# Moving the later SBUF pools to multiples of 512 bytes, and the second chunk of narrow weight units to byte 2048

## The chip, the cores and the metric

The kernel runs on one core of a Trainium2 chip (trn2). The metric is the device time of one execution in microseconds, as the median of several runs. Before the change it is 2218.45 us (three runs, 2217.58 to 2218.74).

A core has a matrix engine (TensorE, PE in the profile), two engines for elementwise work (VectorE, DVE, and ScalarE, ACT), a general one (GpSimd, POOL) and a queue processor (SyncE, SP). All read an on-chip memory, SBUF, of 128 partitions; an operand's place in it is the byte at which it begins in each partition. TensorE writes to PSUM, an accumulation memory. A matmul has a stationary operand, which a weight load (LDWEIGHTS, PEld in the profile) brings into the array, and a moving operand, whose columns stream through it.

## The reference, cut to what matters

The program is a two-layer decoder trunk on 256 tokens of width 2048, all in float32:

```python
for i in range(DEPTH):                       # 2 layers
    if i == N_A_LAYERS:                      # i == 1
        fk, fv, fc = fox_shared_kv(x, fox_kv_norm, fox_w_kv, fox_b_f)
    mk, mv = memory_kv(mem_n, mem_w_kv[i])
    h = rmsnorm(x, norm_mix[i])
    if i < N_A_LAYERS:  x = x + gla_mixer(h, mk, mv, gla_w_in[i], ..., gla_w_out[i])
    else:               x = x + fox_mixer(h, fk, fv, fc, mk, mv, fox_w_in[j], fox_w_out[j])
    h = rmsnorm(x, norm_ffn[i])
    x = x + conv_ffn(h, ffn_w_up[i], ffn_conv_w[i], ffn_conv_b[i], ffn_w_down[i])
return rmsnorm(x, norm_final)
```

`conv_ffn` multiplies by a 2048 x 11264 matrix, applies a causal convolution of width 3 over the tokens, a gate, and multiplies by a 5632 x 2048 matrix. The mixers are a gated linear attention (GLA, 4 heads, keys of 256, values of 384) and a forgetting attention (FoX, 12 heads of 128), each with four heads that attend to 256 memory tokens. Nearly all arithmetic is the product of 256 tokens with some 104 million weights, each of which is read once from the main memory.

## The kernel before, in words

**Arithmetic.** Every weight and every activation is split into a high and a low part (`hi`, `lo`), both of a type called float32r that the matrix engine takes in one pass. A product is three matmuls: high by high, low by high, high by low. The tokens stand as the stationary operand, 128 tokens by 128 channels at a time, and the weights move, up to 512 columns at a time.

**Weights.** The weights lie in the main memory as units (`_layout`, line 114 on). A unit of most panels holds two chunks of 128 input channels (`per` = 2) by n output columns, side by side in each partition: chunk 0 in columns 0 to n - 1, chunk 1 in columns n to 2n - 1. `split_unit` (line 209) issues one DMA for a unit into a buffer `raw` (four of them), one ACT instruction that rounds it into `whi`, and one DVE instruction that subtracts to give `wlo`. `whi` and `wlo` have four buffers of 4096 bytes (`NUNIT` = 1024 columns) each, so PE can be up to four units behind.

**Panels.** A panel is a block of output columns. `panel_tm` (line 307) makes one step for each of its eight units: 12 matmuls, over two blocks of 128 tokens, two chunks, and the three products. n is 512 in most panels. It is 384 in four of them (three of the GLA value panels, `("gv", 1)` to `("gv", 3)`, and `("fv", 3)`). It is 400 in `("gv", 0)` (384 values and 16 gate columns, 8 units), and 388 in `("fv", 0)` to `("fv", 2)` (24 units). Only 400 and 388 are no multiples of P = 128; there chunk 1 begins at byte 1600 and 1552 of its buffer.

**FFN.** `pair_steps` (line 377) runs the products of the two FFNs. Some pairs of its units are computed with seven block products in place of eight. The sums of token blocks which that needs are stationary operands; they lie in tiles `usum` and `dsum`, made by `held` (line 1375) in the pool that is handed to `ffn`. For the hidden activations 20 tiles are needed (`RING`), 16 of them in the constant pool. The other four are, in the first FFN, parts of two tiles of the constant pool (`moremk`, `moremv`, line 1635), and in the second FFN four tiles `more` in its own pool `store` (line 1703). `rows_tm` (line 338), which runs the last panels of the second FFN, reads the `more` tiles too.

**Where the tiles lie.** Pools are laid one behind the other. The constant pool and the weight pool come first. All tiles that matmuls read there (the activations `A`, `B`, `mix`, the `moremk` and `moremv` tiles, `whi`, `wlo`) begin at multiples of 512 bytes: `whi` and `wlo` fill bytes 101,376 to 134,143. The pool `small` (tiles of norms and softmax sums, `sm`, line 156) begins at byte 134,144, which is 262 x 512, and takes 5,504 bytes. So each pool that opens behind it (`load`, `near`, `gla`, `stash`, `turn1`, `fnear`, `fox`, `turn2`, `store`) begins at byte 139,648 or is stacked on one that does, and that is 272 x 512 + 384. The tiles `usum`, `dsum` and `more` all lie at 384 bytes behind a multiple of 512, and each 128 x 128 stationary operand (512 bytes in a partition) in them too. `x` and `raw` lie in a pool of the other end (`rear`) and are not concerned.

**Order.** PE's instructions run in the order in which the program gives them, within bounds: a scheduler orders all engines' instructions by priority (`tc.high_priority(offset=AHEAD)` brings a unit's load and split forward by 300 places) and by modelled costs (`schedule_with_timeline_sim=True` where the kernel is built). `tc.issue_after` ties some instructions behind others.

Of the kernel before, what the change touches and what calls it, by code (L numbers as in the profile page):

```python
# [13 lines left out]
F32 = mybir.dt.float32  # L14
F32R = mybir.dt.float32r
I32 = mybir.dt.int32
AF = mybir.ActivationFunctionType
ALU = mybir.AluOpType
PSUM = bass.MemoryType.PSUM

P = 128
# [22 lines left out]
NUNIT = 1024  # L44
# [102 lines left out]
def _trunk(ctx: ExitStack, tc: tile.TileContext, xt, xtok, memt, wp, wgu, gns, gfin, cnv, par, msk, out):  # L147
    nc = tc.nc
    where, _ = _layout()
    V, S, TE = nc.vector, nc.scalar, nc.tensor  # L150
# [3 lines left out]
    rear = ctx.enter_context(tc.tile_pool(name="rear", bufs=1, side="right"))  # L154
    x = [rear.tile([P, 2, 512], F32, name=f"x{f}") for f in range(4)]
    sm = ctx.enter_context(tc.tile_pool(name="small", bufs=2))
    pacc = ctx.enter_context(tc.tile_pool(name="pacc", bufs=4, space=PSUM))
    dram = ctx.enter_context(tc.tile_pool(name="turnd", bufs=1, space=bass.MemoryType.DRAM))
    pwork = ctx.enter_context(tc.tile_pool(name="pwork", bufs=1, space=PSUM))
# [8 lines left out]
    part = const.tile([P, P], F32, name="part")[:, :C_N]  # L168
# [15 lines left out]
    loads, casts, lows, ends, last_mm, sent = [], [], [], [], [], []  # L184
# [5 lines left out]
    def work(tag, bufs=1):  # L190
        return pwork.tile([P, 512], F32, name="ps_" + tag, tag=tag, bufs=bufs)
# [17 lines left out]
    def split_unit(unit, pieces=1, before=None):  # L209

        off, kcs, n = unit
        w = len(kcs) * n
        with tc.high_priority(offset=AHEAD):
            raw = rear.tile([P, NUNIT], F32, name="raw", tag="raw", bufs=4)
            hi = wpool.tile([P, NUNIT], F32R, name="whi", tag="whi", bufs=4)
            lo = wpool.tile([P, NUNIT], F32R, name="wlo", tag="wlo", bufs=4)
            src = wp[off : off + P * w].rearrange("(p n) -> p n", p=P)
            for i in range(pieces):
                s = slice(i * w // pieces, (i + 1) * w // pieces)
                loads.append(nc.sync.dma_start(raw[:, s], src[:, s]))  # L220
            for i in range(pieces):
                s = slice(i * w // pieces, (i + 1) * w // pieces)
                if before is not None:
                    before(i)
                casts.append(S.activation(hi[:, s], raw[:, s], AF.Copy))  # L225
                lows.append(V.tensor_tensor(lo[:, s], raw[:, s], hi[:, s].bitcast(F32), ALU.subtract))  # L226
        return hi, lo
# [6 lines left out]
    def panels_fm(keys, src, evacs, turns, between=None):  # L234

        units = [where[key] for key in keys]

        acc = [[work("s", 2) if p == 1 else pacc.tile([P, 512], F32, name="acc", tag="acc") for _ in range(2)]
               for p in range(len(keys))]
        base = min(min(u[1]) for u in units[0])  # L240
        ready = {}
        for at, (p, u, low) in enumerate(turns):
            if (p, u) not in ready:
                ready[p, u] = split_unit(units[p][u])
                if u == 1 and between is not None:
                    between()
            end = all(t[0] != p for t in turns[at + 1 :])
            w = ready[p, u][low]
            for j, kc in enumerate(units[p][u][1]):
                both = src[kc - base]  # L250
                for c in range(2):
                    s = slice(j * 256 + c * P, j * 256 + (c + 1) * P)
                    if low:
                        mm = TE.matmul(acc[p][c][:, :T], w[:, s], both[:, 0, :], start=False, stop=end and j == 3)  # L254
                    else:
                        mm = TE.matmul(acc[p][c], w[:, s], both, start=u == j == 0, stop=end and j == 3)  # L256
            if end:
                ends.append(mm)
                with tc.high_priority(offset=2 * AHEAD if len(keys) > 1 and p == 0 else 0):
                    for c in range(2):  # L260
                        evacs[p](c, acc[p][c])
# [46 lines left out]
    def panel_tm(key, src, evac, second=False):  # L308

        units = where[key]
        n = units[0][2]
        base = min(min(u[1]) for u in units)
        acc = []
        end = len(units) - 1

        def step(i):
            if i == 0:
                acc.extend(work("s", 2) if second else pacc.tile([P, 512], F32, name="acc", tag="acc")  # L320
                           for _ in range(2))
            ready = split_unit(units[i])
            passes = [(b, low) for low in range(2) for b in range(2)]
            if i == end:
                passes.sort()
            for b, low in passes:
                for j, kc in enumerate(units[i][1]):
                    for part in range(2 - low):
                        mm = TE.matmul(acc[b][:, :n], src[kc - base][:, part, b * P : (b + 1) * P],  # L329
                                       ready[low][:, j * n : (j + 1) * n], start=i == low == part == j == 0,  # L330
                                       stop=i == end and low == 1 and j == len(units[i][1]) - 1)
                if i == end and low:
                    ends.append(mm)
                    evac(b, acc[b][:, :n])
            last_mm.append(mm)

        return step
# [405 lines left out]
    with tc.tile_pool(name="load", bufs=1) as lp:  # L743
# [48 lines left out]
        def mem_keys(l, z):  # L792
            with tc.issue_after(loads[-1].ins):
                keys_far.pop(0)(flat(z))
            with tc.issue_after(lows[-1].ins):
                for k in range(MEM_H):
                    V.tensor_tensor(by_run(mk[l][:, k, :]), z[:, :, k], by_run(nrm.row()), ALU.mult)

        step = panel_tm(("mk", 0), bufA, turn_out(sq_y, keys_far.append))
        xf = [lp.tile([P, T], F32, name=f"xf{i}") for i in range(KC)]  # L800
        for u in range(8):
# [11 lines left out]
        with tc.issue_after(nrm.made.ins):  # L813
            for i in range(KC):
                split(bufB, i, xf[i], gain("mix0", i))
        step = panel_tm(("mk", 1), bufA, turn_out(sq_y, keys_far.append))
        for u in range(8):
            step(u)
            if u == 3:
# [3 lines left out]
                for f in range(4):  # L823
                    for b in range(2):
                        nx.add(f, b)
        step = panel_tm(("mv", 1), bufA, mv_out(1))
        for u in range(8):
            step(u)
# [743 lines left out]
    def preparing(name, dst, pool, far, kept=None, tag="blk", queue=nc.sync):  # L1572

        n = StreamNorm()
        blocks, rooms, turned_blocks = {}, {}, []
        away, landed = [], []  # L1580

        def land(z=None):

            f, back = away.pop(0)
            if z is None:
                z = pool.tile([P, 4, 4, 2, 32], F32, name="turn", tag="turn", bufs=2) if kept is None else kept[f]
            with tc.issue_after((loads if queue is nc.sync else sent)[-1].ins):
                back(flat(z))
            landed.append((f, z))

        def take():

            f, z = landed.pop(0)
            with tc.issue_after(casts[-1].ins):
                for k in range(4):
                    split_turned(dst, 4 * f + k, z, name)

        def then(f, b):
            n.add(f, b)
            with tc.high_priority(offset=AHEAD):  # L1600
                if b == 0:
                    blocks[f] = rooms[f]() if f in rooms else pool.tile([P, 4, 4, 2, 32], F32, name="blk", tag=tag, bufs=2)
                y = blocks[f]
                turned_blocks.append(V.transpose(y[:, :, :, b, :],
                                                 x[f][:, b, :].rearrange("p (k c i) -> p c k i", c=4, i=32)))
                if b:
                    with tc.issue_after(sent[-1].ins) if queue is nc.gpsimd else nullcontext():
                        away.append((f, far_away(far, flat(y), T, queue)))

        n.rooms = then.rooms = rooms  # L1610
        then.turned = turned_blocks
        n.land = then.land = land
        n.take = then.take = take
        return n, then

    n = gla(nx)
# [20 lines left out]
    with tc.tile_pool(name="turn2", bufs=1) as tp:  # L1637
        n, then = preparing("ffn1", bufA, tp, dram)
# [136 lines left out]
```

## Time and profile before

| what | value |
|---|---|
| median of three runs | 2218.45 us (2217.58 to 2218.74) |
| the profiled execution's own time | 2218.68 us |
| its span, first to last instruction | 2216.9 us |
| PE busy | 2205.0 us, 99% of the span, 10323 matmuls |
| DVE, ACT, POOL busy | 1784.6, 1420.0, 136.9 us (81%, 64%, 6%) |
| mean granted clock of PE | 0.999 |
| moved by DMA | 515.41 MB, 232 GB/s on the mean |

The profiled execution stands 0.23 us above the median of the runs. PE's busy time is the union of its matmuls, and each matmul's record lasts longer than the distance to the next one's start, since they are pipelined. So PE counts as busy even where its matmuls come at a slower pace; what a matmul costs is the distance between starts, which the timeline gives: start, duration of a merged row, count.

### The profile page before, as it was taken

The page shows a single profiled execution, that of the slowest core. Times are in us where ns is not written, and L with a number is a line of the kernel's source. Part 1 is how long each engine was busy: PE and PEld are TensorE (multiplying, and loading weights), DVE is VectorE, ACT ScalarE, POOL GpSimd, SP SyncE. Part 2 cuts the span into 40 slices and gives each one's busy share as a digit, 9 for nine tenths or more (in the row PEclk, how much of TensorE's full clock was granted, in tenths as well). Part 3 has the DMA queues.
Part 4 walks back from the last instruction along what each step waited for, and adds up shares of the span by engine and source line. Part 5 has one row for each costly group of instructions (what it writes and reads, how often), then busy time and mean ns, then how long its engine had stood idle before and what let it go on. Part 6 is the DMA issues. An engine that isn't in the chain of part 4 may idle for free.

```text
span 2216.9 us, 30032 instructions
## 1 busy us (share of the span) xinstructions
PE 2205.0 (99%) x10323; PEld 1854.6 (84%) x10323; DVE 1784.6 (81%) x2640; ACT 1420.0 (64%) x2255; POOL 136.9 (6%) x257
## 2 busy tenths in 40 slices
PE   9999999999999999999999999999999999999998
PEld 7888888888888888888888998888888888888886
DVE  7768977688897878888978669668888788888896
ACT  6655664566787568656765555455787657665874
POOL 0000000001100000001110000000101000100000
PEclk9999999999999999999999999999999999999999
DMA  9877567877777567667678767777777757766674
GB/s 339 253 228 225 185 199 221 262 233 254 229 242 262 186 221 242 223 223 253 219 246 264 231 199 243 228 241 247 217 238 247 243 183 249 232 247 216 223 258 150
DMA packets 165713, 515.41 MB, mean 232 GB/s; under 512 B 20716, under 2 KB 41976, under 8 KB 165560
## 3 DMA queue, kind: packets, MB, share of 16 engines
q1 hardware_dynamic: 148488, 460.99, 63.1%
q0 software_dynamic: 16496, 51.71, 7.6%
q8 instruction: 81, 1.33, 0.2%
q10 hardware_dynamic: 576, 0.79, 0.1%
q14 instruction: 72, 0.59, 0.1%
HBM read 469.62 MB, written 43.79 MB: 232 GB/s over the span
## 4 chain that ended last, share of the span: by engine, by line
PE 99%; DMA 0%; DVE 0%; ACT 0%; SPq 0%; issue 0%; DVEq 0%
PE acc L403 30%; PE acc L329 26%; PE ps_s L403 15%; PE ps_o L403 8%; PE ps_t L403 7%; PE acc L301 3%; PE acc L256 3%; PE acc L359 2%; PE ps_s L329 2%; PE acc L254 1%; PE ps_s L1014 0%; DMA raw<-wp 0%; PE ps_o L687 0%; PE ps_s L687 0%; PE ps_o L1242 0%; PE ps_s L1287 0%
## 5 line engine op out<-in xcount | busy, mean ns | idle before, releaser
L226 DVE TENSOR_TENSOR wlo<-raw,whi 128x1024 fp32r<-128x1024 f32 (+4 forms) x739 | 875.6, 1193 | 255.7 <-ACT whi L225 236.3
L225 ACT ACTIVATE whi<-raw 128x1024 fp32r<-128x1024 f32 (+4 forms) x739 | 763.7, 1041 | 442.2 <-PE acc L329 158.5
L329 PE MATMUL acc<-whi,B 128*128 128x512 f32 (+3 forms) x1248 | 291.8, 370 | 0.0
L373 ACT ACTIVATE whi<-raw 128x1024 fp32r<-128x1024 f32 (+1 forms) x136 | 129.8, 954 | 189.3 <-PE acc L403 70.4
L329 PEld LDWEIGHTS acc<-whi,B 128*128 128x128 f32 x1248 | 227.0, 188 | 28.0
L374 DVE TENSOR_TENSOR wlo<-raw,whi 128x1024 fp32r<-128x1024 f32 (+1 forms) x136 | 147.8, 1089 | 58.9 <-ACT whi L373 55.9
L403 PE MATMUL acc<-whi,mix 128*128 128x512 f32 x764 | 194.8, 389 | 0.0
L403 PE MATMUL acc<-whi,B 128*128 128x512 f32 x750 | 192.7, 389 | 0.0
L403 PEld LDWEIGHTS acc<-whi,mix 128*128 128x128 f32 x764 | 143.4, 188 | 30.0
L403 PEld LDWEIGHTS acc<-whi,B 128*128 128x128 f32 x750 | 140.8, 188 | 29.4
L329 PE MATMUL acc<-wlo,B 128*128 128x512 f32 (+3 forms) x624 | 158.5, 369 | 0.0
L329 PEld LDWEIGHTS acc<-wlo,B 128*128 128x128 f32 x624 | 114.6, 188 | 14.5
L1393 ACT ACTIVATE tap<-yzu,cw 128x256 f32<-128x256 f32 x264 | 123.6, 532 | 2.8 <-DMA yzu<-far 2.7
L1393 ACT ACTIVATE tap<-fvt,cw 128x256 f32<-128x256 f32 x264 | 123.6, 533 | 1.9 <-DMA fvt<-far 1.9
L1400 DVE TENSOR_TENSOR tap<-tap,tap 128x1024 f32<-128x1024 f32 x88 | 107.0, 1216 | 1.1 <-ACT tap L1393 1.0
L403 PE MATMUL acc<-wlo,mix 128*128 128x512 f32 x382 | 107.4, 389 | 0.0
L403 PE MATMUL acc<-wlo,B 128*128 128x512 f32 x375 | 107.1, 389 | 0.0
L403 PE MATMUL ps_s<-whi,mix 128*128 128x512 f32 x386 | 105.9, 389 | 0.0
L403 PE MATMUL ps_s<-whi,B 128*128 128x512 f32 x342 | 93.3, 389 | 0.0
L403 PEld LDWEIGHTS ps_s<-whi,mix 128*128 128x128 f32 x386 | 72.5, 188 | 15.2
L403 PEld LDWEIGHTS acc<-wlo,mix 128*128 128x128 f32 x382 | 71.8, 188 | 15.0
L403 PEld LDWEIGHTS acc<-wlo,B 128*128 128x128 f32 x375 | 70.4, 188 | 14.7
(498 smaller groups left out, 3792.6 us busy)
## 6 DMA issues: line engine op xcount, KB each, us to landing
raw<-wp SPq DMA_DIRECT2D x743, 512.0 KB, 4.5
fvt<-far POOLq DMA_DIRECT2D x100, 128.0 KB, 5.4
raw<-wp SPq DMA_DIRECT2D x32, 384.0 KB, 3.5
far<-yu POOLq DMA_DIRECT2D x22, 512.0 KB, 5.6
far<-yzu POOLq DMA_DIRECT2D x22, 512.0 KB, 5.2
yzu<-far POOLq DMA_DIRECT2D x88, 128.0 KB, 5.5
raw<-wp SPq DMA_DIRECT2D x24, 388.0 KB, 4.1
x<-xtok SPq DMA_DIRECT2D x8, 512.0 KB, 7.2
```

The costliest lines, as they stand in the source:

```text
L225: casts.append(S.activation(hi[:, s], raw[:, s], AF.Copy))
L226: lows.append(V.tensor_tensor(lo[:, s], raw[:, s], hi[:, s].bitcast(F32), ALU.subtract))
L254: mm = TE.matmul(acc[p][c][:, :T], w[:, s], both[:, 0, :], start=False, stop=end and j == 3)
L256: mm = TE.matmul(acc[p][c], w[:, s], both, start=u == j == 0, stop=end and j == 3)
L301: mm = TE.matmul(acc[b][:, :n], src[kcs[j] - base][:, part, b * P : (b + 1) * P], w, start=u == 0 and low == part == j == 0, stop=u == end ...
L329: mm = TE.matmul(acc[b][:, :n], src[kc - base][:, part, b * P : (b + 1) * P], ready[low][:, j * n : (j + 1) * n], start=i == low == part = ...
L359: mm = TE.matmul(acc[b][:, :n], src[kc - base][:, part, b * P : (b + 1) * P], w, start=i == low == part == j == 0, stop=i == end and low = ...
L373: casts.append(S.activation(hi[:, :n], src, AF.Copy))
L374: lows.append(V.tensor_tensor(lo[:, :n], src, hi[:, :n].bitcast(F32), ALU.subtract))
L403: r = TE.matmul(bank[name], x, w, start=name not in begun, stop=last)
L1393: S.activation(by_run(taps[i][:, s, c, i:]), zs[slot][:, :, 2 * c + s], AF.Copy if i else AF.Identity, bias=0.0 if i else w[3], scale=w[2 ...
L1400: V.tensor_tensor(taps[0], taps[0], taps[n][:, :, :, :T], ALU.add)
```

## The change

Two things are changed, and nothing in the arithmetic.

1. A tile `even` of 32 float32 columns (128 bytes in a partition) that nobody writes or reads is put first into the pool `small`. The pool's other tiles move up by 128 bytes, and it ends at byte 139,776 = 273 x 512. Every pool behind it moves up by 128 bytes.
2. In units whose n is no multiple of 128 (400 and 388), `split_unit` writes chunk 1 of `whi` and `wlo` to column 512, byte 2048, and `panel_tm` reads it there. The ACT and the DVE instruction stay one each, with the same elements; their output (and DVE's second input) is now two runs of n columns, 512 apart. The load is the same. `room` is NUNIT // 2 = 512 for such a unit and n for all others.

```diff
     sm = ctx.enter_context(tc.tile_pool(name="small", bufs=2))
+    sm.tile([P, 32], F32, name="even", tag="even", bufs=1)
...
                 loads.append(nc.sync.dma_start(raw[:, s], src[:, s]))
+            if n % P:
+                a, b, c = (t.rearrange("p (j m) -> p j m", j=len(kcs))[:, :, :n] for t in (raw[:, :w], hi, lo))
+                casts.append(S.activation(b, a, AF.Copy))
+                lows.append(V.tensor_tensor(c, a, b.bitcast(F32), ALU.subtract))
+                return hi, lo
             for i in range(pieces):
...
         n = units[0][2]
+        room = NUNIT // len(units[0][1]) if n % P else n
         base = min(min(u[1]) for u in units)
...
                         mm = TE.matmul(acc[b][:, :n], src[kc - base][:, part, b * P : (b + 1) * P],
-                                       ready[low][:, j * n : (j + 1) * n], start=i == low == part == j == 0,
+                                       ready[low][:, j * room : j * room + n], start=i == low == part == j == 0,
                                        stop=i == end and low == 1 and j == len(units[i][1]) - 1)
```

## The prediction

> **What bounds the kernel now.** I read the page first, then the work of each engine by stage, then PE's groups by tile, and last the timeline of single stretches of PE, which gives its pace.
>
> ```profile
> span 2216.9 us, 30032 instructions
> ...
> PE 2205.0 (99%) x10323; PEld 1854.6 (84%) x10323; DVE 1784.6 (81%) x2640; ACT 1420.0 (64%) x2255; POOL 136.9 (6%) x257
> ...
> PE 99%; DMA 0%; DVE 0%; ACT 0%; SPq 0%; issue 0%; DVEq 0%
> ...
> PE acc L301 <- ACT whi L225: 1.3, 1, 1.3
> ...
> 400.00:800.00 400.00, 400.00 (x1763) 330.64 (x1762) 329.01 (x422) 263.05 (x400) 27.41 (x50) 1.00 0.71 233
> ...
> 1600.00:2000.00 400.00, 400.00 (x1760) 330.21 (x1759) 337.43 (x398) 276.27 (x414) 35.13 (x64) 1.00 0.69 231
> ```
>
> The chain that ended last is PE for 99%. Among PE's waits the one that a split caused lasted 1.3 us, at the start. In the two stretches of 400 us, which hold most of both FFNs, PE is busy throughout at the full granted clock (the 1.00), while DVE has 329 and 337 us of work and ACT 263 and 276. So the time is the number of matmuls times their pace. Only what changes that pace, or makes a matmul wait, counts. The pace is not the same everywhere:
>
> ```profile
> 887.43 1.98 PE L403 MATMUL acc<-whi,moremk 128*128 128x512 f32 x8
> ...
> 898.31 0.39 PE L403 MATMUL acc<-whi,mix 128*128 128x512 f32 x1
> ...
> 1926.97 2.03 PE L403 MATMUL acc<-whi,more 128*128 128x512 f32 x8
> ...
> 1938.13 0.62 PE L403 MATMUL acc<-whi,mix 128*128 128x512 f32 x2
> ```
>
> Between the first two starts lie 4 units of 12 matmuls, with `moremk` and `moremv` as stationary operands: 10.88 us / 48 = 226.7 ns each. Between the last two lie the same 48 matmuls of the second FFN, from the same line, with `more`: 11.16 / 48 = 232.5 ns. The first tiles begin at multiples of 512 bytes, the second 384 bytes behind one. The difference is 5.8 ns.
>
> **The change part by part.** It adds and removes no matmul, load or DMA, and no wait; ACT and DVE keep one instruction each per unit. Four things remain.
>
> *(a) Stationary operands of 512-column matmuls.* Those that move from 384 bytes behind to a multiple of 512 are the tiles `usum`, `dsum` and `more`; the groups that carry the count, with `moremk` as the mate that is already in place:
>
> ```profile
> L403 PE MATMUL acc<-whi,usum 128*128 128x512 f32 x100 | 29.8, 395 | 0.0
> ...
> L403 PE MATMUL acc<-wlo,usum 128*128 128x512 f32 x50 | 17.9, 397 | 0.0
> ...
> L403 PE MATMUL ps_s<-whi,usum 128*128 128x512 f32 x80 | 23.2, 395 | 0.0
> ...
> L403 PE MATMUL ps_s<-wlo,usum 128*128 128x512 f32 x40 | 13.6, 396 | 0.0
> ...
> L403 PE MATMUL acc<-whi,dsum 128*128 128x512 f32 x32 | 9.1, 396 | 0.0
> ...
> L403 PE MATMUL ps_t<-wlo,dsum 128*128 128x512 f32 x4 | 1.6, 397 | 0.0
> ...
> L403 PE MATMUL ps_s<-whi,more 128*128 128x512 f32 x32 | 8.9, 395 | 0.0
> ...
> L359 PE MATMUL acc<-spare,more 128*128 128x512 f32 x24 | 5.9, 395 | 0.0
> ...
> L359 PE MATMUL acc<-wlo,more 128*128 128x512 f32 x8 | 2.2, 394 | 0.0
> ...
> L403 PE MATMUL acc<-whi,moremk 128*128 128x512 f32 x16 | 4.0, 389 | 0.0
> ```
>
> All groups of `usum` have 312 matmuls, of `dsum` 96, of `more` 192: 600. Each group's count times its mean less 389 gives 2.10 us for `usum`, 0.66 for `dsum` and 1.10 for `more`, 3.85 us in sum, or 6.4 ns a matmul. A record's excess is the pace's excess: `more` is 394 to 396 against 389 here, and 5.8 ns in the timeline. At 5.8 for all, 600 give 3.5 us. I take 3.85, since `usum` has the longest records, and 3.5 to 3.9 as its bounds. All of it is on the path, since PE is. What would be late next is the split; DVE's 63 to 71 us of slack in 400 us is far above the 0.7 us that PE gains in such a stretch.
>
> *(b) The moving operand of 388 and 400 columns.* 24 units of 388 and 8 of 400, 12 matmuls each: 288 and 96, half of them with chunk 1. Their pace, beside that of 384 columns, whose chunks lie at multiples of 512 already:
>
> ```profile
> 95.30 0.52 PE L329 MATMUL acc<-whi,B 128*128 128x400 f32 x2
> ...
> 112.74 0.62 PE L329 MATMUL acc<-whi,B 128*128 128x512 f32 x2
> ...
> 1266.79 1.56 PE L329 MATMUL acc<-whi,B 128*128 128x388 f32 x8
> ...
> 1283.77 0.51 PE L329 MATMUL acc<-whi,B 128*128 128x384 f32 x2
> ...
> 1300.42 0.39 PE L256 MATMUL acc<-mix,whi 128*128 128x512 f32 x1
> ...
> L329 PE MATMUL acc<-whi,B 128*128 128x384 f32 x256 | 51.9, 336 | 0.0
> L329 PE MATMUL acc<-whi,B 128*128 128x388 f32 x192 | 38.6, 340 | 0.0
> ```
>
> The starts bound three panels of 96 matmuls: 17.44 us or 181.7 ns at 400 columns, 16.98 or 176.9 at 388 (the last of three), 16.65 or 173.4 at 384. From 384 to 512 columns the pace grows from 173.4 to 226.7, that is 0.416 ns a column, so 388 and 400 columns should cost 175.1 and 180.1. They cost 1.8 and 1.6 ns more; by the records of all three panels, where others run in between, 388 columns cost 340 - 336 - 1.7 = 2.3 ns more. That is 288 x 2.3 + 96 x 1.6 = 0.82 us, or 0.67 by the one panel. Whether the offset of chunk 1 makes it, or the odd width, the trace before can't say, since its rows don't tell the chunks apart. So the gain lies between 0 and 0.8 us. A loss is excluded as far as the place goes: chunk 0 and every 384-column chunk lie at such places now. I take 0.8, as the rows in place are the nearest, and they show no excess.
>
> *(c) The split in two runs.* Its instructions now:
>
> ```profile
> L225 ACT ACTIVATE whi<-raw 128x1024 fp32r<-128x1024 f32 x673 | 708.0, 1060 | 384.6 <-PE acc L329 112.0 <-PE acc L403 84.5 <-PE ps_t L403 83.0
> ...
> L225 ACT ACTIVATE whi<-raw 128x776 fp32r<-128x776 f32 x24 | 20.4, 854 | 21.5 <-PE acc L329 18.0 <-DMA raw<-wp 3.2
> ...
> L226 DVE TENSOR_TENSOR wlo<-raw,whi 128x776 fp32r<-128x776 f32 x24 | 23.0, 963 | 18.5 <-ACT whi L225 17.9 <-PE acc L329 0.6
> ...
> 1242.80:1272.00 29.20, 29.20 (x169) 29.08 (x168) 15.97 (x22) 17.62 (x25) 0.00 (x0) 1.00 0.78 247
> ```
>
> A unit takes PE 12 x 177 = 2.12 us, and 29.2 us hold 13.8 of them. ACT works 17.62 us there, 1.28 a unit, and DVE 1.16. Nothing in the trace shows such a split; one run or two, it has the same 776 elements, so I cost it between 0 and, as if each run were an instruction of its own, the fixed part of one more. That part comes from the rows of 1024 and 776 columns, 1060 and 854 ns on ACT: 0.83 ns a column leaves 854 - 645 = 209 ns; DVE's is alike. ACT then stands at 1.49 us of 2.12, so PE hides it; without that cover it would be 32 x 0.2 = 6.7 us.
>
> *(d) All else that moves.* The attention's operands move into place with the pools, and `dg`, the moving operand of 14 matmuls in `small`, out of it, to 128 bytes behind.
>
> ```profile
> L687 PE MATMUL ps_s<-kv,mqp x48: 274/281/288, 171.0 to 1339.5; 128*128 128x256 f32 x48
> L687 PE MATMUL ps_o<-pts,kv x48: 274/282/387, 214.0 to 1372.3; 128*128 128x256 f32 x48
> L254 PE MATMUL acc<-mix,wlo x192: 277/283/469, 1304.1 to 1399.6; 128*128 128x256 f32 x192
> ...
> L1007 PE MATMUL ps_s<-gq,gk 128*128 128x128 f32 x16 | 2.4, 274 | 0.0
> L1244 PE MATMUL ps_o<-z,fvt 128*128 128x128 f32 x24 | 4.6, 273 | 0.0
> L1014 PE MATMUL ps_s<-gdd,ks 128*64 128x96 f32 x128 | 6.9, 249 | 0.0
> L1014 PE MATMUL ps_s<-gdd,gqk 128*64 128x96 f32 x64 | 4.3, 255 | 0.0
> ```
>
> With 256 columns the median is 281 out of place as stationary operand (`mqp`), 282 out of place as moving operand (`pts`), and 283 in place (L254). With 128 columns it is 273 out of place (`fvt`, stationary) and 274 for tiles that stay (`gk`). The gain there is 0. `gdd` has no mate; its 192 matmuls are worth 1.1 us at most, by (a)'s 5.8 ns, and 0 by the rows above, which are nearer in shape. `dg` loses at most 14 x 5.8 ns = 0.08 us. I take 0 for all of it.
>
> **Sum.** 3.85 + 0.8 = 4.65 us off the profiled execution's 2218.68 us, that is 2214.0. Off the median, 0.23 lower, it is 2213.8 us. 0.2% of the median, about what a measurement of this kernel can tell from no change, is 4.4 us, so the forecast lies close to that bound.
>
> The Trainium skill has a rule that speaks against this sum. "SBUF — State Buffer", section "Door 1: The DMA port swizzle", says that SBUF works in lines of 16 bytes and that crossing to a new line is what costs. Byte offsets of 384 and 1552 are whole lines, so by that rule both edits change nothing, and the sum would be 2218.45 us. The trace's 232.5 against 226.7 ns for the same matmuls disagrees, unless something else than the offset makes it.
>
> **The rivals.**
> - *Only the stationary part comes back.* The 1.6 to 2.3 ns of (b) belong to the width. For it: `pts`, out of place and moving, costs nothing at 256 columns. 2218.45 - 3.85 = 2214.6 us.
> - *The change doesn't do what it says.* What costs 5.8 ns is not the offset but that `usum`, `dsum` and `more` lie far up, above byte 139,648, while all stationary tiles at 389 ns lie below 101,376. Place and offset go together in the trace. Against it: `mqp` lies as far up and costs nothing at 256 columns. Then only (b) is left: 2217.6 to 2218.45, say 2218.2.
> - *The scheduler orders otherwise, and the kernel is slower.* It places by modelled costs; if a two-run split is priced otherwise, the interleave of splits and evacuations from `("gv", 0)` on shifts, and units come late. PE's one such wait cost 1.3 us. It takes the gain away at 4.65 / 1.3 = 3.6 waits, and makes the kernel 0.2% slower at (4.65 + 4.4) / 1.3, that is 7, where 32 units are split anew and all later ones follow: eight waits give 2218.45 - 4.65 + 10.4 = 2224.2 us. For it: DVE waits for ACT in 17.9 of its 18.5 idle us before these splits, so a shift of ACT goes on to DVE. Against it: PE waited nowhere for a split after the start. Two waits would give 2216.4.
> - *More comes back.* `gdd`'s matmuls gain too: with half of their bound, 0.6 us, it is 2213.2 us. For it: (a). Against it: the other short matmuls, which gain nothing.
>
> **How the numbers follow.** Both parts come back and nothing else: 0.50, at 2213.8 us, its own range 2213.4 to 2214.6 (the bounds of (a), 3.5 to 3.9, and most of (b), with a spread of 0.3 us between medians, half of what the three runs show). More comes back: 0.10. Only the stationary part: 0.12. No effect of the offset: 0.08. Order shifted, slower: 0.12. Order shifted by a wait or two: 0.08. The range 2213.0 to 2218.3 leaves out the slower case and little else. Faster by over 0.2% (below 2214.0) takes 0.37 of the first case, the whole second, 0.02 of the third, which lies 0.6 us off that bound, and 0.01 of the last: 0.50. Slower is 0.12. The rest, 0.38, is within 0.2%.
>
> **What would show it.** In the profile after, `usum`, `dsum` and `more` should have 389 ns as minimum and median alike, as `moremk` has; at 394 to 397 the place makes it. A panel of 388 should take 16.81 us and of 400 17.29; at 16.98 and 17.44 the width makes it. Casts of 776 stay near 854 ns, up to 1063. PE's waits should still be the one of 1.3 us. The prediction is wrong if PE waits for `whi` elsewhere, or if DVE's or ACT's busy time grows by more than the 32 splits can.

## The result and the profile after

The changed kernel takes 2213.26 us as the median of 12 runs (2212.19 to 2214.42), beside 2217.76 us for the kernel before in 12 runs of the same comparison (2217.34 to 2218.74). The ratio is 0.9979, with a 95% interval of 0.9971 to 0.9987: 4.5 us less, with 2.9 to 6.4 us as its bounds. The profiled execution took 2213.36 us, 5.32 less than the one before.

From the page of the kernel after: the span, then busy time, share and instructions of each engine.

```profile
span 2211.5 us, 30032 instructions
...
PE 2200.9 (100%) x10323; PEld 1854.7 (84%) x10323; DVE 1784.5 (81%) x2640; ACT 1420.5 (64%) x2255; POOL 136.5 (6%) x257
```

The instructions are as many as before, and every engine issues them in the same order, with as many wait instructions. PE's busy time fell by 4.1 us, DVE's and ACT's by nothing to speak of. The span fell by 5.4 us, so 1.3 us more than PE's work. That is in the main one wait at the start; of PE's waits in the kernel after (line, releaser, us in total, times, longest) only this is left:

```profile
PE ps_o L183 <- DVE B L180: 1.5, 1, 1.5
```

The wait of 1.3 us for `whi` at the start, which the profile before has, is gone. The rest is pace. The tiles that moved, by the groups of the kernel after (minimum, median and maximum of a record in ns, first and last start):

```profile
L410 PE MATMUL acc<-whi,usum x100: 388/390/390, 475.2 to 2091.0; 128*128 128x512 f32 x100
...
L410 PE MATMUL acc<-whi,dsum x32: 388/390/390, 727.2 to 2135.4; 128*128 128x512 f32 x32
...
L410 PE MATMUL ps_s<-whi,more x32: 388/390/390, 1956.5 to 2146.3; 128*128 128x512 f32 x32
...
L366 PE MATMUL acc<-spare,more x24: 388/390/390, 2191.4 to 2199.4; 128*128 128x512 f32 x24
```

PE's timeline after, at the places that were shown of before (start, duration of the merged row, count):

```profile
94.23 1.07 PE L336 MATMUL acc<-whi,B 128*128 128x400 f32 x5
...
111.52 0.86 PE L336 MATMUL acc<-whi,B 128*128 128x512 f32 x3
...
1264.15 1.58 PE L336 MATMUL acc<-whi,B 128*128 128x388 f32 x8
...
1281.11 1.55 PE L336 MATMUL acc<-whi,B 128*128 128x384 f32 x8
...
1297.76 2.01 PE L262 MATMUL acc<-mix,whi 128*128 128x512 f32 x8
...
1923.45 1.98 PE L410 MATMUL acc<-whi,more 128*128 128x512 f32 x8
...
1934.33 1.98 PE L410 MATMUL acc<-whi,mix 128*128 128x512 f32 x8
```

Set beside the starts of before, these rows say where the time went:

| stretch | before, us | after, us | saved in it, us | saved up to its end, us |
|---|---|---|---|---|
| up to the panel of 400 columns | 95.30 | 94.23 | 1.07 | 1.07 |
| that panel, 96 matmuls | 17.44 | 17.29 | 0.15 | 1.22 |
| up to the last panel of 388 | 1154.05 | 1152.63 | 1.42 | 2.64 |
| that panel, 96 matmuls | 16.98 | 16.96 | 0.02 | 2.66 |
| the panel of 384, 96 matmuls | 16.65 | 16.65 | 0.00 | 2.66 |
| up to the four units with `more` | 626.55 | 625.69 | 0.86 | 3.52 |
| those units, 48 matmuls | 11.16 | 10.88 | 0.28 | 3.80 |
| up to the end of the span | | | 1.6 | 5.4 |

The first 1.07 us arise at the start, where the wait of 1.3 us is gone. The 48 matmuls with `more` now come every 10.88 / 48 = 226.7 ns, as those with `moremk` do. The panel of 400 columns stands at 180.1 ns a matmul. The panel of 388 is where it was, at 176.7 ns.

The casts of 776 columns and the short matmuls, by the groups of the kernel after (busy us, mean ns of one, idle time before):

```profile
L224 ACT ACTIVATE whi<-raw 128x776 fp32r<-128x776 f32 x24 | 20.4, 853 | 21.9 <-PE acc L336 17.8 <-DMA raw<-wp 3.7
...
L225 DVE TENSOR_TENSOR wlo<-raw,whi 128x776 fp32r<-128x776 f32 x24 | 23.0, 964 | 18.5 <-ACT whi L224 17.9 <-PE acc L336 0.6
...
L1021 PE MATMUL ps_s<-gdd,ks 128*64 128x96 f32 x128 | 6.9, 249 | 0.0
...
L1021 PE MATMUL ps_s<-gdd,gqk 128*64 128x96 f32 x64 | 4.3, 255 | 0.0
```

All four are as before, within 1 ns: two output runs cost ACT and DVE nothing, and `gdd`'s matmuls did not gain.

### The profile page after: what moved, and what is told of

Read it like the earlier page. It is cut to its first block, busy times and chain, and to the rows that moved or that the text cites. A ratio compares the mean times of both kernels' runs of the same rounds, so it can differ in the third digit from the quotient of the medians.

```text
span 2211.5 us, 30032 instructions
## 1 busy us (share of the span) xinstructions
PE 2200.9 (100%) x10323; PEld 1854.7 (84%) x10323; DVE 1784.5 (81%) x2640; ACT 1420.5 (64%) x2255; POOL 136.5 (6%) x257
## 4 chain that ended last, share of the span: by engine, by line
PE 99%; DMA 0%; DVE 0%; ACT 0%; SPq 0%; issue 0%; DVEq 0%
PE acc L410 30%; PE acc L336 26%; PE ps_s L410 15%; PE ps_o L410 8%; PE ps_t L410 7%; PE acc L307 3%; PE acc L262 3%; PE acc L366 2%; PE ps_s L336 2%; PE acc L260 1%; PE ps_s L1021 0%; PE ps_o L694 0%; DMA raw<-wp 0%; PE ps_s L694 0%; PE ps_s L1294 0%; PE ps_s L1067 0%
## 5 line engine op out<-in xcount | busy, mean ns | idle before, releaser
L232 DVE TENSOR_TENSOR wlo<-raw,whi 128x1024 fp32r<-128x1024 f32 (+2 forms) x707 | 845.4, 1204 | 236.1 <-ACT whi L231 216.6
L231 ACT ACTIVATE whi<-raw 128x1024 fp32r<-128x1024 f32 (+2 forms) x707 | 736.0, 1049 | 410.0 <-PE acc L336 130.5
L336 PEld LDWEIGHTS acc<-whi,B 128*128 128x128 f32 x1248 | 226.9, 188 | 28.0
```

## The experiments

The theory at this point: a 512-column matmul loses 5.8 ns when its stationary operand lies off some multiple of bytes, and the tile `even` takes that away. Its rivals: it is another property of those high places; it is the split of the units; it is the start.

**1. The tile alone.** The kernel before with the tile `even`, units packed as before.

```diff
     sm = ctx.enter_context(tc.tile_pool(name="small", bufs=2))
+    sm.tile([P, 32], F32, name="even", tag="even", bufs=1)
```

> The tile of 128 bytes alone; units of 388 and 400 columns stay as before. Theory (the offset of the stationary operand sets the pace): the 600 matmuls with usum, dsum and more go to 389 or 390 ns, 3.85 us off the kernel before (2217.76), so about 2213.9; with the 1.2 us that the profile after gained at the start as well, 2212.9 to 2213.5. The 388 and 400 panels stay at 176.9 and 181.7 ns a matmul. Rival (the two edits need each other, or the gain is elsewhere): above 2215.

Measured: 2213.66 us beside 2218.32, ratio 0.9978 (0.9969 to 0.9987). Its `usum` records, and its panels of 388 and 400 columns (groups: busy us, mean ns):

```profile
L404 PE MATMUL acc<-whi,usum x100: 389/389/389, 475.0 to 2091.5; 128*128 128x512 f32 x100
```

```profile
L330 PE MATMUL acc<-whi,B 128*128 128x388 f32 x192 | 38.5, 339 | 0.0
...
L330 PE MATMUL acc<-whi,B 128*128 128x400 f32 x64 | 13.1, 344 | 0.0
```

The tile alone gives the whole gain that a comparison of medians can show.

**2. The second chunk alone.** The changed kernel without the tile.

```diff
     sm = ctx.enter_context(tc.tile_pool(name="small", bufs=2))
-    sm.tile([P, 32], F32, name="even", tag="even", bufs=1)
```

> The second chunk at byte 2048 alone; the later pools stay 384 bytes behind a multiple of 512. By the panels of the profile after, the 96 matmuls of 400 columns gain 1.6 ns each (181.6 to 180.1), 0.15 us, and the 288 of 388 columns 0.2 ns, 0.06 us: about 2217.5 against 2217.76, no change that can be measured. usum, dsum and more stay at 393 to 397 ns. The prediction had 0.8 us for this part, 2217.0. A wait of PE at line 307 of about 1.3 us at the start should be there again if the place of the load pool makes it.

Measured: 2217.86 us beside 2218.32, ratio 0.9999 (0.9991 to 1.0008). The same rows:

```profile
L409 PE MATMUL acc<-whi,usum x100: 390/395/404, 474.9 to 2094.2; 128*128 128x512 f32 x100
```

```profile
L335 PE MATMUL acc<-whi,B 128*128 128x388 f32 x192 | 38.5, 339 | 0.0
...
L335 PE MATMUL acc<-whi,B 128*128 128x400 f32 x64 | 13.0, 341 | 0.0
```

`usum` is slow again. Byte 2048 takes 3 ns off the records of 400 columns and none off those of 388: in the first experiment, with the packed chunk, they stand at 339 as well. So (b) is real for 400 and nearly nothing for 388.

**3. Multiples of 256.** The kernel before, with single buffers for four tags of one or two columns in the pool `small`. The pools behind it then begin 256 bytes behind a multiple of 512.

```diff
-        junk = sm.tile([P, 1], F32, name="junk", tag="root")
+        junk = sm.tile([P, 1], F32, name="junk", tag="root", bufs=1)
...
-            part = sm.tile([P, 1], F32, name="fp", tag="fp")
+            part = sm.tile([P, 1], F32, name="fp", tag="fp", bufs=1)
...
-            v = sm.tile([P, 2], F32, name="fv", tag="fv")
+            v = sm.tile([P, 2], F32, name="fv", tag="fv", bufs=1)
...
-            r = sm.tile([P, 1], F32, name="root", tag="root")
+            r = sm.tile([P, 1], F32, name="root", tag="root", bufs=1)
...
-            c = sm.tile([P, 1], F32, name="fc", tag="fc")
+            c = sm.tile([P, 1], F32, name="fc", tag="fc", bufs=1)
```

> The kernel before with four tags of the pool small cut to one buffer, so that the later pools begin 256 bytes behind a multiple of 512 in place of 384. If an operand of 512 bytes has to begin at a multiple of 512 (it crosses such a boundary at any other offset), usum, dsum and more stay at 393 to 397 ns and the time at 2217.8, less up to 1.2 us for the start. If multiples of 256 do, they go to 389 or 390 and the time to about 2213.9. The cut buffers touch the last 10 us alone, at most 0.5 us.

Measured: 2213.03 us beside 2218.32, ratio 0.9976 (0.9967 to 0.9986). The stretch with `more` in this kernel's timeline:

```profile
1922.57 1.98 PE L403 MATMUL acc<-whi,more 128*128 128x512 f32 x8
...
1933.45 1.98 PE L403 MATMUL acc<-whi,mix 128*128 128x512 f32 x8
```

That is 10.88 us again, 226.7 ns: multiples of 256 bytes are enough for the stationary operand.

**4. The load pool back.** The changed kernel with 384 bytes more ahead of the tiles of the pool `load`, which carries the memory tokens at the start. It asks whether the wait at the start comes and goes with that pool's place.

```diff
     with tc.tile_pool(name="load", bufs=1) as lp:
+        lp.tile([P, 96], F32, name="back")
```

> The changed kernel, but a tile of 384 bytes ahead of the first tiles of the pool load puts that pool, and it alone, 384 bytes behind a multiple of 512 again. If the place of the first loads makes the wait at the start, PE waits about 1.3 us at line 307 and the time is 2214.5 against 2213.3 for the changed kernel; if that wait differs from execution to execution, the time stays at 2213.3. Nothing else moves.

Measured: 2213.23 us beside 2218.32, ratio 0.9978 (0.9969 to 0.9987). In its profile PE waits 1.5 us for `B` at the start and nowhere else, just as in the changed kernel. In experiment 2, where that pool lies 384 bytes behind as well, it waits 0.6 us for `whi`. The place of that pool alone doesn't make the wait.

**5. The stationary operands out of place.** The changed kernel with two small tiles of the constant pool made wider and narrower, so that `A`, `B`, `mix`, `moremk` and `moremv` begin 128 bytes behind a multiple of 512, while `whi`, `wlo` and all later pools stay.

```diff
-    gains = const.tile([P, G_N], F32, name="gains")
+    gains = const.tile([P, P], F32, name="gains")[:, :G_N]
...
-    part = const.tile([P, P], F32, name="part")[:, :C_N]
+    part = const.tile([P, 96], F32, name="part")[:, :C_N]
```

> The changed kernel with the tiles of the constant pool from A0 on 128 bytes further, so that nearly all stationary operands (A, B, mix, moremk, moremv) begin 128 bytes behind a multiple of 512, low in SBUF; whi and wlo, the moving operands, and all later pools stay where the change put them. Theory: their 512-column matmuls, some 8,000, slow by 5.8 to 6.4 ns each, 46 to 51 us in sum, and the narrower panels by up to 5 us more: 2260 to 2270. Rival (the cost belonged to the later pools' place): 2213.3.

Measured: 2260.63 us, ratio 1.0192 (1.0178 to 1.0207), 47.4 us above the changed kernel. In this kernel's timeline the two stretches of the prediction have changed roles:

```profile
904.00 2.03 PE L410 MATMUL acc<-whi,moremk 128*128 128x512 f32 x8
...
915.15 2.02 PE L410 MATMUL acc<-whi,mix 128*128 128x512 f32 x8
...
1964.72 1.98 PE L410 MATMUL acc<-whi,more 128*128 128x512 f32 x8
...
1975.61 2.03 PE L410 MATMUL acc<-whi,mix 128*128 128x512 f32 x8
```

With `moremk` and `moremv`, low down and out of place, 48 matmuls take 11.15 us (232.3 ns); with `more`, high up and in place, 10.89 (226.9). So it is the offset and not the height. Counted over the groups there are 8,707 matmuls of 512 columns; all but the 600 that stay, some 8,100, at 5.6 to 5.8 ns are 45 to 47 us, nearly all of the loss. The panels of 384, 388 and 400 columns lose some 2 us more.

In a few of these matmuls the tiles that moved are the moving operand. `panels_fm` (L260 and L262), which computes some of the panels, exchanges the roles: there the weights stand, and the activations `A` and `mix` move. With 512 columns its group `acc<-A,whi` goes from 390 ns in the changed kernel to 395 here. Of the 600 too, 24 have a moving operand in a tile of `A` (`acc<-spare,more`), and go from 389 to 394.

**6. The moving operand out of place.** The changed kernel with one tile narrower ahead of the weight pool and `even` wider behind it: `whi` and `wlo` begin 384 bytes behind a multiple of 512, everything else stays. They are the moving operand in the panels and the FFNs, and the stationary one in `panels_fm`.

```diff
-    sm.tile([P, 32], F32, name="even", tag="even", bufs=1)
+    sm.tile([P, 64], F32, name="even", tag="even", bufs=1)
...
-    part = const.tile([P, P], F32, name="part")[:, :C_N]
+    part = const.tile([P, 96], F32, name="part")[:, :C_N]
```

> The changed kernel with whi and wlo 128 bytes lower, so that every moving operand begins 384 bytes behind a multiple of 512; all stationary operands stay. If the moving operand's offset costs what the misplaced half of the 400-column matmuls cost (1.6 ns in the mean of both chunks, so 3.2 each), the 512-column matmuls, some 8,600, cost 27 us more: about 2240. If only the stationary operand's offset counts: 2213.3 to 2214, and the 400-column panel's gain was something else.

Measured: 2268.13 us, ratio 1.0224 (1.0210 to 1.0239), 54.9 us above the changed kernel: twice what was expected. Its timeline, the panel of 400 columns, the three of 388 (the middle one has matmuls of other lines in it), that of 384, and the stretch with `more`:

```profile
96.38 1.63 PE L336 MATMUL acc<-whi,B 128*128 128x400 f32 x8
...
113.98 1.33 PE L336 MATMUL acc<-whi,B 128*128 128x512 f32 x5
...
1261.26 1.55 PE L336 MATMUL acc<-whi,B 128*128 128x388 f32 x8
...
1277.90 1.55 PE L336 MATMUL acc<-whi,B 128*128 128x388 f32 x8
...
1295.33 1.58 PE L336 MATMUL acc<-whi,B 128*128 128x388 f32 x8
...
1312.40 1.57 PE L336 MATMUL acc<-whi,B 128*128 128x384 f32 x8
...
1329.25 3.89 PE L262 MATMUL acc<-mix,whi 128*128 128x512 f32 x16
...
1970.37 2.03 PE L410 MATMUL acc<-whi,more 128*128 128x512 f32 x8
...
1981.57 2.03 PE L410 MATMUL acc<-whi,mix 128*128 128x512 f32 x8
```

384 columns: 16.85 us, 175.5 ns, 2.1 above those in place. 400: 17.60, 183.3 ns, 3.2 above. 512: 11.20 / 48 = 233.3 ns, 6.6 above. But 388 columns don't fit in between: the first panel takes 16.64 us, 173.3 ns, which is 3.4 less than in place, and the last 17.07, 177.8, which is 1.1 more. Two panels of the same width, with their operands at the same places, differ; why is open.

At 256 columns there is nothing. The group of L260 has the stationary `wlo` out of place here, the moving `mix` out of place in experiment 5, and both in place in the kernel after; in this order:

```profile
L260 PE MATMUL acc<-mix,wlo 128*128 128x256 f32 x192 | 26.5, 287 | 0.0
```

```profile
L260 PE MATMUL acc<-mix,wlo 128*128 128x256 f32 x192 | 26.5, 286 | 0.0
```

```profile
L260 PE MATMUL acc<-mix,wlo 128*128 128x256 f32 x192 | 26.7, 288 | 0.0
```

I had taken the 3.2 ns that a step of 400 columns showed for all widths. At 512 columns the price is twice that. (The 3.2 ns came from a chunk 1 at byte 1600, 64 bytes behind a multiple of 256; here it is 128 bytes.)

**7. The second chunk at byte 1792.** The changed kernel with 448 columns of room, which is 7 x 256 bytes.

```diff
-                a, b, c = (t.rearrange("p (j m) -> p j m", j=len(kcs))[:, :, :n] for t in (raw[:, :w], hi, lo))
+                a, b, c = (t.rearrange("p (j m) -> p j m", j=len(kcs))[:, :, :n] for t in (raw[:, :w], hi[:, :896], lo[:, :896]))
...
-        room = NUNIT // len(units[0][1]) if n % P else n
+        room = 448 if n % P else n
```

> The changed kernel with the second chunk of units of 400 and 388 columns at byte 1792, a multiple of 256 and not of 512. If multiples of 256 are enough for the moving operand, as they were for the stationary one, 400 columns run at 180.1 ns flat and 388 at 176.6 alternating between 172 and 182; if it needs 512, 400 columns go back to 181 to 182 with spread. The time stays within 0.2 us of the changed kernel either way.

Measured, one run: 2213.08 us beside 2219.17. Its panel of 400 columns:

```profile
94.51 1.61 PE L336 MATMUL acc<-whi,B 128*128 128x400 f32 x8
...
111.80 1.32 PE L336 MATMUL acc<-whi,B 128*128 128x512 f32 x5
```

17.29 us, as at byte 2048: 256 is enough for the moving operand too. In its list of waits stands `whi` with 1.0 us at the start, and yet the run is no slower than the others; its panel of 400 columns begins only 0.28 us later than in the changed kernel:

```profile
PE acc L307 <- ACT whi L231: 1.0, 1, 1.0
```

**8. Sixty-four bytes short.** The changed kernel with `even` half as wide: the later pools begin 448 bytes behind a multiple of 512.

```diff
-    sm.tile([P, 32], F32, name="even", tag="even", bufs=1)
+    sm.tile([P, 16], F32, name="even", tag="even", bufs=1)
```

> The changed kernel with a tile of 64 bytes in place of 128, so that the later pools begin 448 bytes behind a multiple of 512 (192 behind one of 256). If any offset from 256 costs alike, usum, dsum and more run at 394 to 397 ns again, 3.5 to 3.9 us, and the time is near 2217. If the cost grows with the distance to the next multiple of 256 (64 bytes here, 128 before), they run at about 392 and the time is near 2215.

Measured, one run: 2216.33 us beside 2219.17. In its timeline the 48 matmuls with `more` take 10.98 us, 228.8 ns, while `moremk` stays at 10.88:

```profile
886.23 1.98 PE L410 MATMUL acc<-whi,moremk 128*128 128x512 f32 x8
...
897.11 1.98 PE L410 MATMUL acc<-whi,mix 128*128 128x512 f32 x8
...
1925.53 2.00 PE L410 MATMUL acc<-whi,more 128*128 128x512 f32 x8
...
1936.51 1.98 PE L410 MATMUL acc<-whi,mix 128*128 128x512 f32 x8
```

So in this stretch 64 bytes off cost 2.1 ns, and 128 bytes off 5.6 to 5.8. It is not a matter of in place or out of place alone. Over all matmuls of a tile the distances between starts are 2.5 ns longer than in the changed kernel for `more`, 3.3 for `dsum` and 4.2 for `usum` (without one wait of 0.4 us), some 2.1 us in sum. The median of the `usum` records in the largest group is 392 ns. That is the second case expected; the rest of the 3.1 us by which this one run is slower than the changed kernel is not explained.

**9. Even panels.** The changed kernel with `("fv", 0)` to `("fv", 3)` cut so that the 12 additional columns make 396 of the first and the others have 384.

```diff
-FV_PARTS = ((0, 376), (376, 764), (764, 1152), (1152, 1536))
+FV_PARTS = ((0, 384), (384, 768), (768, 1152), (1152, 1536))
```

> The changed kernel with the four value panels cut at 396, 384, 384 and 384 columns in place of 388, 388, 388 and 384. At 173.4 ns for 384 columns, and 180.1 (as 400) or 178.4 (no steps) for 396, the four panels take 96 x (178.4 to 180.1 + 3 x 173.4) against 96 x (3 x 176.6 + 173.4): 0.27 to 0.44 us less, about 2212.9 against 2213.3 for the changed kernel.

Measured: 2213.06 us beside 2218.04, ratio 0.9977 (0.9968 to 0.9987). Its panel of 396 columns:

```profile
1229.31 1.60 PE L336 MATMUL acc<-whi,B 128*128 128x396 f32 x8
...
1246.58 1.55 PE L336 MATMUL acc<-whi,B 128*128 128x384 f32 x8
```

17.27 us, 179.9 ns: 396 columns cost as much as 400. Against three panels of 388 and one of 384 that is 17.27 + 3 x 16.65 = 67.22 us instead of 3 x 16.96 + 16.65 = 67.53, a gain of 0.3 us. It can't be told from the changed kernel by medians.

**10 and 11. Other widths.** The changed kernel with other cuts of the same panels: 400, 388, 376, 384 in the one, 404, 392, 380, 372 in the other.

```diff
-FV_PARTS = ((0, 376), (376, 764), (764, 1152), (1152, 1536))
+FV_PARTS = ((0, 388), (388, 776), (776, 1152), (1152, 1536))
```

> The changed kernel with the four value panels of the second layer cut at other columns: 400, 388, 376 and 384 columns in place of 388, 388, 388 and 384; the same columns in sum. In the profile after, matmuls of 388 columns alternate between 172 and 182 ns, 176.6 in the mean, although both chunks lie at multiples of 512. If the width counts in steps of 8 columns, 388 cost as 392 (0.416 ns a column from 173.4 at 384: 176.7) and 376 cost 170.1, without alternation. In steps of 16 columns, 376 would cost as 384, 173.4, and 388 as 400, 180.1. Without steps, 170.1 and 175.1. 400 is 180.1 by each.

```diff
-FV_PARTS = ((0, 376), (376, 764), (764, 1152), (1152, 1536))
+FV_PARTS = ((0, 392), (392, 784), (784, 1164), (1164, 1536))
```

> The changed kernel with the four value panels of the second layer cut at 404, 392, 380 and 372 columns. So far, in place, 376 columns cost 173.3 ns (as 384), 396 cost 180.0 (as 400), and 388 cost 176.6, halfway between 384 and 400. If columns count in steps of 16 and a rest of 4 costs half a step: 404 at 183.4, 392 at 180.1, 380 at 173.4, 372 at 170.1. If 388 is a case of its own and steps of 16 hold elsewhere: 404 at 186.7 and 372 at 173.4. Without steps: 181.7, 176.7, 171.7 and 168.4.

Measured, one run each: 2213.96 us beside 2218.04, and 2212.82 beside 2219.45. From the timeline of the first, 376 and then 384 columns:

```profile
1264.75 1.54 PE L336 MATMUL acc<-whi,B 128*128 128x376 f32 x8
...
1281.38 1.55 PE L336 MATMUL acc<-whi,B 128*128 128x384 f32 x8
...
1298.02 3.83 PE L262 MATMUL acc<-mix,whi 128*128 128x512 f32 x16
```

From the second, 404, then the start of 392, then 380 and 372:

```profile
1229.59 1.62 PE L336 MATMUL acc<-whi,B 128*128 128x404 f32 x8
...
1247.08 1.58 PE L336 MATMUL acc<-whi,B 128*128 128x392 f32 x8
...
1264.56 1.55 PE L336 MATMUL acc<-whi,B 128*128 128x380 f32 x8
...
1280.99 1.52 PE L336 MATMUL acc<-whi,B 128*128 128x372 f32 x8
...
1297.31 3.79 PE L262 MATMUL acc<-mix,whi 128*128 128x512 f32 x16
```

Each panel has 96 matmuls. Beside the straight line through 384 columns (173.4 ns) and 512 (226.7), all in place:

| columns | 372 | 376 | 380 | 384 | 388 | 396 | 400 | 404 |
|---|---|---|---|---|---|---|---|---|
| ns a matmul | 170.0 | 173.2 | 171.1 | 173.4 | 176.7 | 179.9 | 180.1 | 182.2 |
| above the line | 1.6 | 3.1 | -0.6 | 0 | 1.6 | 1.5 | 0 | 0.5 |

(The panel of 392 has matmuls of other lines in it; apart from those its starts are 177.3 ns apart, 0.6 above the line.) None of the rules expected gives all of these. The excess of 388 columns is thus there with both operands in place, so an offset doesn't make it. It is no step of 16 columns, since 380 and 404 lie near the line. Nor does it go with the width alone: the first panel of 388 in experiment 6 lies 1.8 ns below the line. What it is stays open.

## Why the prediction was right, and where it was not

*What bounds.* Right. PE's work is the span but for the start, and a change of pace of a few ns shows in the time with nothing between: +5.8 ns on some 8,100 matmuls is +47 us in experiment 5.

*(a) The stationary operands: right.* The forecast was 389 ns for all three tiles and 3.85 us. The records are 388 to 390, the pace of `more` fell from 232.5 to 226.7 ns, and the tile alone brings the gain (experiment 1). Added up from the distances between starts, the kernel before spends 2.10 us more than the changed one on the matmuls with `usum`, 0.65 on those with `dsum` and 1.14 on those with `more`: 3.89 us. Experiment 5 excludes the rival that the height of the place makes it. One reading behind that rival was wrong: not all stationary tiles at 389 ns lay below byte 101,376, for `whi`, at 101,376 to 134,143, is stationary in `acc<-A,whi` of line 256, and its records were 389 ns too. The rule of the Trainium skill that spoke against the sum ("SBUF — State Buffer", section "Door 1: The DMA port swizzle") is that of lines of 16 bytes, where crossing to a new line costs. It does not carry over to TensorE's operands here: 128, 384 and 448 bytes are whole lines, and as offsets they cost 2.1 to 6.6 ns a matmul of 512 columns.

*(b) The moving operand: half right, and its larger term mis-sized.* The 400 columns did what was forecast: 17.29 us for the panel, which is 96 x 1.6 ns = 0.15 us. For 388 columns the term was 288 x 2.3 ns = 0.66 us; the panel after is 16.96 us where 16.81 was forecast, 0.02 us less than before, which for three panels is 0.06. The step that failed is "I take 0.8, as the rows in place are the nearest, and they show no excess". The rows in place were of 384 and 512 columns, and the line between them was taken for the price of 388. The excess over that line was no sign of the offset, for it is there in place too. Nor were the two offsets alike: chunk 1 lay 64 bytes behind a multiple of 256 at 400 columns (byte 1600), and 16 bytes at 388 (byte 1552), so even a real price of the offset may have been smaller at 388. "A loss is excluded as far as the place goes" was not safe either, since the first panel of 388 in experiment 6 is faster out of place than in place. Here the rival *only the stationary part comes back* was nearly right: (a) and (b) together come to 3.85 + 0.21 = 4.1 us. PE's busy time lost as much, though that agreement is closer than it need be: the busy times of experiments 1 and 3, which differ in little, are 2201.3 and 2200.1 us.

*(c) and (d): right.* Casts at 853 and 964 ns, `gdd` at 249 and 255. The rival *more comes back* falls with that, and the one with another order of the engines too, since the order is the same and no wait of PE for a split was added.

*What would show it.* "PE's waits should still be the one of 1.3 us" was wrong, and not by the change. That wait is 1.3 us in the one profile of before. In the profiles of kernels that differ from the changed one only far from the start it is 0, 0.5 or 1.0 us, and it is 0 in experiment 3, which works its units as the kernel before does. Up to there all of them do the same work in the same order, so the likely reading is that it differs from one execution to the next; no kernel was profiled twice to show it. So of the 5.3 us between the two profiled executions, 1.3 are that wait and 4.1 the change (the two are 0.1 more than the difference).

*The sum.* 2213.8 was forecast, 2213.26 measured. That the time is lower, although (b) brought 0.6 us less, is no merit of the working: the kernel before itself stands at 2217.76 in this comparison, 0.69 below the median of three from which the sum was made, so the difference of medians is 4.5 us against 4.65 forecast. The paces account for 4.1 of it; the remaining 0.4 lie within the interval of 2.9 to 6.4 us. The ratio lies at the bound of what can be told from no change, as forecast: 0.9979, with 0.998 inside its interval.

## What to carry to other kernels

Where PE is busy throughout, read its pace from the distance of starts in the timeline, for mates that differ in one thing alone, here the place of the stationary operand; the busy share says 99% either way. Then look where every operand of the wide matmuls begins, modulo 256 bytes, the small pools ahead of them included: a tile of 128 bytes that nobody uses is worth 4 us here, and moving the common operands the wrong way costs 47 to 55. An excess over a straight line between two widths is not yet an excess over what that width costs: measure the width itself in place before giving the excess to a cause.

## What was not expected of the hardware

- A moving operand off its multiple costs about as much as a stationary one: 6.6 against 5.8 ns at 512 columns. The price depends on the columns: 0 at 256 (experiment 5), 2.1 at 384, 3.2 at 400, 6.6 at 512 (experiment 6), but between -3.4 and 1.1 at 388. Why is not known; no run here shows the reads of the array.
- With both operands in place, pace is not a straight line in the columns: 376 columns cost as much as 384 (16.63 and 16.64 us a panel), and 396 as much as 400 (17.27 and 17.29).
- The amount depends on the distance: for the stationary operand 64 bytes short of a multiple of 256 cost 2.1 to 4.2 ns, 128 bytes 5.6 to 5.8 in the stretches shown, and 256 bytes nothing (226.7 ns). Other distances were not tried for it.
- PE's first wait for weights is 0 to 1.3 us in these profiles, up to a quarter of the whole effect, with nothing in the kernels found to set it. Single executions of this kernel can't decide on 1 us; the pace of a stretch can decide on 0.1.
